# Queries and keys of both attention branches: seven quadrant products in place of eight in a transformer layer's input projection

## The chip, the core and the metric

One core of one Trainium2 chip runs the whole layer in one launch. The metric is device time in microseconds (us). The kernel before took 2883.06 us (median of 3 runs, 2879.89 to 2885.41).

Names: PE is TensorE (matrix products; "PEld" is its load of stationary weights), DVE is VectorE, ACT is ScalarE, POOL is GpSimd, SP is SyncE, which here only issues DMAs. SBUF is the on-chip memory with 128 partitions, PSUM the memory that PE writes its sums to. `T` = 1024 tokens, `D` = 1024 features, `TC` = 256 context tokens, `P` = 128.

## What is computed

The reference is one layer of a diffusion transformer with two attention branches. Cut to what matters here:

```
x  = layer_norm(x, ...) * (1 + sc1) + sh1          # 1024 tokens x 1024
xc = layer_norm(ctx, ...) * (1 + sc1c) + sh1c      # 256 tokens x 1024
p, pc = x @ w_in, xc @ w_in                        # w_in: 1024 x 11264
qr, kr, vr, gr, qd, kd, vd, gate_r, gate_d = split(p)
qr, kr, qd, kd = rope(qr), rope(kr), rope(qd), rope(kd)
... chunked retention on qr, kr, vr; differential attention on qd, kd, vd;
... gates, output projection, layer norm, gated feed-forward, layer norm
```

The context rows of the keys (`kr`, `kd`) are projected too and not rotated; queries have no context rows. All products keep close to fp32 precision: each operand is split into a high part (`h`, rounded to the matmul type fp32r) and a low part (`l` = x - h), and three matmuls h*h + h*l + l*h stand for one (`mm3`).

## The kernel before, in words

The program is written as straight Python loops. A scheduler orders the instructions of each engine before the launch, by its own estimate of times, and each engine then runs its list in that order. So an instruction that waits holds up all that is behind it on its engine.

**First stage (L324 to L397).** Eight blocks of 128 tokens of x are loaded, normalised on DVE and POOL, transposed on PE into `xn` (features on partitions, 8 tiles k of 128 x 1024 tokens). Then, for each k, `mod_both` loads 1 MB of `w_mod` by SP and makes scale and shift; POOL applies them to `xn[:, k]` (L396), and `split` (L84: a copy on ACT, a subtraction on DVE) makes `xH[:, k]` and `xL[:, k]` (L397). These stay in SBUF for all projections.

**Projections (L435 to L658).** The columns of `w_in` are taken in groups of 256. For one group `w_cols` (L233) loads two raw tiles `wraw` of 128 x 1024 (four k tiles of 256 columns each) and splits them into the ring of weight tiles `wh`, `wl` (3 raw buffers, 6 of each split tile). `proj_T` (L456) makes one half of a group, 128 columns by 1024 tokens: for each of 8 k tiles, 3 matmuls by 2 cuts of 512 tokens, so 48 matmuls into `px` (PSUM, 128 x 1024); where the context is wanted, 24 more of 256 tokens into `pcx`. A group has two halves. Then `rope` (L468) makes four products of `px` with the cosine and sine tables on DVE, reading PSUM, and POOL does one subtraction and one addition (L477, L478), each 128 x 1024. The differential branch (`proj_dif`, L481) splits each result again and stores it by 16 DMAs of 32 rows on ACT's queue (L497); the retention branch (`proj_ret`, L499) stores it by 2.

The order is QD (4 groups), KD (4, with context), VD (2 groups of 512 columns, `proj_N`, with x as the stationary operand), QR (4), KR (4, with context), VR (4 of 512). The very first group of QD (`proj_first`, L447) takes its k tiles as the first stage delivers them. `context` (L536) normalises the context rows behind the first group; its PE work is 16 transposes into the small PSUM banks (`ptc`). `decays` (L561) makes tables for the retention branch on DVE and ACT.

**Later.** Attention with the projection of the gates beside it, retention, output projections, the feed-forward. The feed-forward's up projection (L1196 to L1400) already makes its products by seven quadrant products in place of eight, with the same order of products 1, 2, 6, 5, 7, 3, 4, a ring of 3 raw and 4 split buffers, four POOL subtractions of 128 x 512 per tile of weights, and copies from PSUM by ACT.

PSUM has two small tiles of one bank each (`small_ps`) and three of two banks (`big_ps`).

Of the kernel before, what the change touches and what calls it, by code (L numbers as in the profile page):

```python
# [16 lines left out]
P = 128  # L17
# [47 lines left out]
def build(nc, tc, A, out, upto=99, dbg=None):  # L65
# [45 lines left out]
    d_row = dram("d_row", [2, D])  # L111

# [159 lines left out]
    def mod_both(pool, raw, segs):  # L272

        tiles = mod_load(raw, segs)
        pm = small_ps("pm")[:, 0:256]
        for s in range(2):
            for i in range(4):
                k = 2 * i + s
                PE.matmul(pm[32 * i:32 * i + 32, :], condT[:, k, :], tiles[k // 4][:, k % 4, :],
                          start=s == 0, stop=s == 1, tile_position=(0, 32 * i))  # L280
        md = pool.tile([P, 256], F32, name="md", tag="md", bufs=2)
# [36 lines left out]
    open_ring("wring1", 3, 6)  # L318
# [4 lines left out]
    with ExitStack() as ph:  # L323
        wp = ph.enter_context(tc.tile_pool(name="p0", bufs=1))  # L324
# [23 lines left out]
        def norm_pair(src, b0, dst, stats):  # L348
            xb = []
            for b in (b0, b0 + 1):  # L350
                t = ring["pool"].tile([P, D], F32, name="xb", tag="wl" if b < 6 else "wh", bufs=ring["bufs"])
# [39 lines left out]
        for k in range(KT):  # L391
            mod_both(wp, lambda i: ring["pool"].tile([P, 1024], F32, name="mr", tag="wh", bufs=ring["bufs"]), (k, 8 + k))
# [42 lines left out]
    with ExitStack() as ph:  # L435
        wp = ph.enter_context(tc.tile_pool(name="p1", bufs=1))
        ropex = ExitStack()
        rp = ropex.enter_context(tc.tile_pool(name="rope", bufs=1, side="right"))
# [8 lines left out]
        def proj_first(ws):  # L447
# [6 lines left out]
            return [(p, None) for p in px]  # L454

        def proj_T(ws, view, want_ctx):  # L456

            px = big_ps("px")
            for k in range(KT):
                mm3(px, (view(ws[k][0]), view(ws[k][1])), (xH[:, k, :], xL[:, k, :]), T, k == 0, k == KT - 1)  # L460
            pc = None
            if want_ctx:
                pc = small_ps("pcx")[:, 0:TC]
                for k in range(KT):
                    mm3(pc, (view(ws[k][0]), view(ws[k][1])), (cH[:, k, :], cL[:, k, :]), TC, k == 0, k == KT - 1)
            return px, pc

        def rope(pa, pb):  # L468
            t = [rp.tile([P, TK if i in (0, 2) else T], F32R, name=f"rp{i}", tag=f"rp{i}", bufs=2 if i in (0, 2) else 1)
                 for i in range(4)]  # L470
            full = t[0], t[2]
            t = [x.bitcast(F32)[:, :T] for x in t]
            tt(t[0], pa, trig["cos"], ALU.mult)
            tt(t[3], pa, trig["sin"], ALU.mult)
            tt(t[1], pb, trig["sin"], ALU.mult)
            tt(t[2], pb, trig["cos"], ALU.mult)
            tt(t[0], t[0], t[1], ALU.subtract, G)  # L477
            tt(t[2], t[2], t[3], ALU.add, G)  # L478
            return full

        def proj_dif(c0, g, dst, want_ctx):  # L481
            if c0 == C_QD and g == 0:
                pq = proj_first(ws0)
            else:
                ws = w_cols(w_in, c0 + g * 256, 256, perm=perm_dif)
                pq = [proj_T(ws, lambda w: w[:, half * P:half * P + P], want_ctx) for half in range(2)]
            for half, l in enumerate(rope(pq[0][0], pq[1][0])):
                h = rp.tile([P, TK], F32R, name="dh", tag="dh", bufs=2)
                split(h[:, :T], l[:, :T], l[:, :T].bitcast(F32))
                n = T  # L490
                if want_ctx:
                    split(h[:, T:], l[:, T:], pq[half][1])
                    n = TK
                for i in range(4):
                    for part, src in ((0, h), (1, l)):
                        r0 = part * 64 + half * 32
                        ST.dma_start(out=dst[4 * g + i, r0:r0 + 32, :n], in_=src[32 * i:32 * i + 32, :n].bitcast(F32))  # L497

        def proj_ret(c0, g, dst, want_ctx):  # L499
            ws = w_cols(w_in, c0 + g * 256, 256)  # L500
            pq = [proj_T(ws, lambda w: w[:, half * P:half * P + P], want_ctx) for half in range(2)]
            for half, tsrc in enumerate(rope(pq[0][0], pq[1][0])):
                ST.dma_start(out=dst[g, half, :, :T], in_=tsrc[:, :T].bitcast(F32))
                if want_ctx:
                    cs = wp.tile([P, TC], F32, name="cs", tag="cs", bufs=2)
                    S.copy(out=cs, in_=pq[half][1])
                    ST.dma_start(out=dst[g, half, :, T:], in_=cs)

# [11 lines left out]
        def proj_N(c0, dst, d0, want_ctx, func):  # L520

            ws = w_cols(w_in, c0, 512)
            for b in range(0, 10 if want_ctx else 8, 2):
# [6 lines left out]
                st = wp.tile([P, 2, 512], F32, name="st", tag="st", bufs=2)  # L530
# [5 lines left out]
        def context():  # L536

            cst = wp.tile([P, 2, 2], F32, name="cst")
            cn = [wp.tile([P, 4, TC], F32, name="cn%d" % i, tag="st", bufs=2) for i in range(2)]
            xb = []  # L540
            for b in range(2):
                t = ring["pool"].tile([P, D], F32, name="xc", tag="wl", bufs=ring["bufs"])
# [18 lines left out]
        def decays():  # L561


            small = wp.tile([P, 1024], F32, name="small", tag="st", bufs=2)
# [61 lines left out]

        with tc.issue_after(turns["mod"]):
            trig_tables("dif")
        for g in range(4):
            with tc.issue_after(turns["mod"]) if g == 1 else ExitStack():  # L630
                proj_dif(C_QD, g, d_qd, False)
            if g == 0:
                with tc.issue_after(turns["mod"]):
                    context()
            if g == 1:
                decays()
        for g in range(4):
            proj_dif(C_KD, g, d_kd, True)
        for g in range(2):
            proj_N(C_VD + g * 512, d_vd, g * 512, True, AF.Copy)  # L640
        trig_tables("ret")
        for g in range(4):
            proj_ret(C_QR, g, d_qr, False)
        for g in range(4):
            proj_ret(C_KR, g, d_kr, True)
        ropex.close()
# [10 lines left out]
        for g in range(4):  # L657
            proj_N(C_VR + g * 512, d_vr, g * 512, True, AF.Copy)  # L658
    bigx.close()
# [852 lines left out]
```

## Time and profile before

| what | value |
|---|---|
| runs | 2883.06 us median (2879.89 to 2885.41) |
| the profiled execution | 2888.07 us, of which its profile spans 2886.3 us |
| PE busy | 2793.8 us, 97% of the span |
| DVE, ACT, POOL busy | 56%, 39%, 28% |
| PE's granted clock | 0.988 of full speed over the span |
| first stage | 0 to about 71 us, its end mixed with the first group |
| QD and KD | about 71 to 247 us |
| VD, QR, KR, VR | about 247 to 359, to 446, to 557, to 780 us |

How to read it: times in the rows are us from the start of the profile's span, those of single instructions ns where marked. "Busy" of PE counts overlapping matmuls, since they are pipelined; the rate at which PE works is the distance of one start to the next. A wait is named by the engine that released it.

### The profile page before, as it was taken

The page shows a single profiled execution, that of the slowest core. Times are in us where ns is not written, and L with a number is a line of the kernel's source. Part 1 is how long each engine was busy: PE and PEld are TensorE (multiplying, and loading weights), DVE is VectorE, ACT ScalarE, POOL GpSimd, SP SyncE. Part 2 cuts the span into 40 slices and gives each one's busy share as a digit, 9 for nine tenths or more (in the row PEclk, how much of TensorE's full clock was granted, in tenths as well). Part 3 has the DMA queues.
Part 4 walks back from the last instruction along what each step waited for, and adds up shares of the span by engine and source line. Part 5 has one row for each costly group of instructions (what it writes and reads, how often), then busy time and mean ns, then how long its engine had stood idle before and what let it go on. Part 6 is the DMA issues. An engine that isn't in the chain of part 4 may idle for free.

```text
span 2886.3 us, 34740 instructions
## 1 busy us (share of the span) xinstructions
PE 2793.8 (97%) x13610; PEld 2327.8 (81%) x13610; DVE 1626.6 (56%) x2139; ACT 1122.6 (39%) x1570; POOL 809.8 (28%) x613
## 2 busy tenths in 40 slices
PE   7999999999999999999998999899998999999997
PEld 5888888888788888888886877788776788888876
DVE  4864243322167766777758775333556555557666
ACT  4321211111144545544546767433345444444221
POOL 3321022100000000000027764234442333337744
PEclk9999999999999999999999999999999999999999
DMA  8755332453233332323233433643321322224421
GB/s 250 212 165 168 125 124 79 132 175 110 70 92 92 112 95 93 108 91 103 65 113 107 140 115 113 236 150 120 118 89 52 110 81 88 81 81 168 138 95 59
DMA packets 261476, 340.18 MB, mean 118 GB/s; under 512 B 15479, under 2 KB 192064, under 8 KB 261312
## 3 DMA queue, kind: packets, MB, share of 16 engines
q1 hardware_dynamic: 222992, 258.50, 28.7%
q10 hardware_dynamic: 38320, 79.46, 7.8%
q8 instruction: 107, 1.75, 0.3%
q14 instruction: 57, 0.47, 0.1%
HBM read 242.73 MB, written 95.17 MB: 117 GB/s over the span
## 4 chain that ended last, share of the span: by engine, by line
PE 81%; DMA 5%; DVE 5%; POOL 3%; ACT 3%; issue 3%; SPq 0%; ACTq 0%; DVEq 0%; POOLq 0%
PE pg L253 18%; PE pxn L253 11%; PE px L253 11%; PE pu L253 8%; PE py L253 8%; PE pyd L253 6%; PE sp L717 5%; PE po L253 4%; PE pxo L253 2%; PE tp L741 2%; PE pcx L253 2%; DMA g<-d_gT 1%; DVE acc L71 1%; PE pS L253 1%; DMA wraw<-in_w_in 1%
## 5 line engine op out<-in xcount | busy, mean ns | idle before, releaser
L71 DVE TENSOR_TENSOR wl<-wraw,wh 128x1024 fp32r<-128x1024 f32 (+1 forms) x233 | 319.8, 1386 | 248.1 <-ACT wh L85 241.5
L85 ACT CAST wh<-wraw 128x1024 fp32r<-128x1024 f32 (+1 forms) x233 | 218.7, 947 | 473.0 <-PE pu L253 107.9
L71 POOL TENSOR_TENSOR rd<-ident,wh 128x512 fp32r<-128x512 f32 x16 | 18.2, 1137 | 860.6 <-ACT wh L85 827.0
L720 DVE TENSOR_SCALAR_CACHE_REDUCE e<-sp 128x1280 f32<-128x1280 f32 x128 | 190.5, 1489 | 107.2 <-PE sp L717 106.5
L82 ACT ACTIVATE e<-e,m 128x1280 f32<-128x1280 f32 x128 | 175.0, 1367 | 184.0 <-DVE e L720 183.6
L71 POOL TENSOR_TENSOR wraw<-wraw 128x512 f32<-128x512 f32 x85 | 148.9, 1752 | 266.7 <-DVE wl L71 254.3
L71 POOL TENSOR_TENSOR rp<-rp,rp 128x1024 f32<-128x1024 f32 x32 | 89.0, 2804 | 379.4 <-DVE rp L71 359.7
L253 PE MATMUL pg<-xH,wh 128*128 128x512 f32 x496 | 194.9, 393 | 0.0
L253 PE MATMUL pg<-xH,wl 128*128 128x512 f32 x496 | 194.7, 393 | 0.0
L253 PE MATMUL pg<-xL,wh 128*128 128x512 f32 x496 | 194.4, 392 | 0.0
L717 PE MATMUL sp<-ks,qd 128*128 128x512 f32 (+1 forms) x768 | 174.4, 362 | 1.5 <-DVE e L720 1.4
L253 PE MATMUL py<-opH,wh 128*128 128x512 f32 x384 | 150.9, 398 | 10.0 <-DVE ga L71 6.0
L253 PE MATMUL px<-xL,wh 128*128 128x512 f32 x512 | 158.2, 390 | 0.0
L253 PE MATMUL px<-xH,wl 128*128 128x512 f32 x512 | 157.7, 389 | 0.0
L253 PE MATMUL px<-xH,wh 128*128 128x512 f32 x512 | 156.8, 391 | 0.0
L253 PE MATMUL py<-opL,wh 128*128 128x512 f32 x384 | 152.1, 396 | 1.0 <-DVE opL L71 1.0
L253 PE MATMUL pxn<-wh,xH 128*128 128x512 f32 x384 | 151.1, 394 | 0.0
L253 PE MATMUL py<-opH,wl 128*128 128x512 f32 x384 | 150.8, 394 | 0.0
L253 PE MATMUL pxn<-wh,xL 128*128 128x512 f32 x384 | 149.6, 390 | 0.0
L253 PE MATMUL pxn<-wl,xH 128*128 128x512 f32 x384 | 149.4, 389 | 0.0
L717 PEld LDWEIGHTS sp<-ks,qd 128*128 128x128 f32 x768 | 129.3, 188 | 24.6 <-DVE e L720 4.2
L81 ACT ACTIVATE st<-pxn 128x1024 f32<-128x1024 f32 x30 | 30.8, 1027 | 235.0 <-PE pxn L253 231.0
(356 smaller groups left out, 7166.7 us busy)
## 6 DMA issues: line engine op xcount, KB each, us to landing
wraw<-in_w_in SPq DMA_DIRECT2D x88, 512.0 KB
wraw<-in_w_up SPq DMA_DIRECT2D x44, 512.0 KB
mr<-in_w_mod SPq DMA_DIRECT2D x32, 512.0 KB
qd<-d_qd SPq DMA_DIRECT2D x128, 128.0 KB
ga<-d_ga SPq DMA_DIRECT2D x24, 512.0 KB
d_u<-u SPq DMA_DIRECT2D x22, 512.0 KB
fl<-d_u SPq DMA_DIRECT2D x22, 512.0 KB
wraw<-in_w_down SPq DMA_DIRECT2D x22, 512.0 KB
```

The source lines that it names most:

```text
L71: eng.tensor_tensor(out=o, in0=a, in1=b, op=op)
L81: return S.activation(out=o, in_=a, func=func, bias=bias, scale=scale)
L82: return S.activation(out=o, in_=a, func=func, bias=bias, scale=scale, accum_out=accum)
L85: S.copy(out=h, in_=x)
L253: PE.matmul(ps[:, c:e], w, m[:, c:e], start=start and i == 0, stop=stop and i == 2, skip_group_check=more)
L717: st["pe"] = PE.matmul(sp[:, a:b], w, r["k"][c][:, a:b], start=part == 0, stop=part == 1).ins
L720: V.tensor_scalar(out=e, in0=sp[:, :TK], scalar1=-0.125, scalar2=None, op0=ALU.mult, op1=ALU.min, accum_out=m)
L741: PE.transpose(tp[:, k, :], a[:, k * P:(k + 1) * P], ident)
```

## The change

What it does:

- 15 of the 16 groups of QD, KD, QR and KR (all but the first) go through `proj_pair`. Both the group (1024 features x 256 columns) and x (1024 features x 1024 tokens) are cut into quadrants: two halves of features, two halves of columns or tokens. Seven products of 512 features, 128 columns and 512 tokens (products 1, 2, 6, 5, 7, 3, 4) make the four quadrants of the result, with sums of quadrants of weights and of x as operands.
- The sums of the weights are made per group on POOL (four subtractions of 128 x 512), and 7 or 8 half tiles are split where 4 were. The sums of x are made in the first stage for k = 4 to 7, two steps on POOL and two on DVE per k, and three splits of 128 x 512 per k. The sum that takes the place of the quadrant a21 is written over `xH` and `xL` after the first group; the original goes out to `d_a21` and comes back before VD.
- Products are put together in SBUF: four copies from PSUM on ACT and three additions on DVE that read PSUM, each 128 x 512. `rope` then reads SBUF and works in place.
- The context rows of KD are stored by DMAs of their own (16 more per group).
- The ring has 4 split buffers in place of 6; several tiles share buffers with others (`xb`, `mr`, `cn`, `xc`, `md`).
- Order: QD, KD, QR, KR, then the reload of `xH`, `xL`, `decays`, VD, VR. `context` comes after the third group in place of the first, and its tiles are in the buffers of the rotation (`rt0`, `rt1`).

With `NP = 0` no gates are made here. Cut to its core:

```diff
-    open_ring("wring1", 3, 6)
+    open_ring("wring1", 3, 4)
...
             split(xH[:, k, :], xL[:, k, :], xn[:, k, :])
+            if k < 4:
+                continue
+            j = k - 4
+            a11, a12, a21, a22 = xn[:, j, t_lo], xn[:, k, t_lo], xn[:, j, t_hi], xn[:, k, t_hi]
+            tt(a11, a11, a21, ALU.subtract, G)
+            split(xs[7][0][:, j, :], xs[7][1][:, j, :], a11)
+            tt(a21, a21, a22, ALU.add)
+            tt(a22, a22, a11, ALU.subtract)
+            split(xs[6][0][:, j, :], xs[6][1][:, j, :], a22)
+            tt(a12, a12, a22, ALU.subtract, G)
+            split(xs[3][0][:, j, :], xs[3][1][:, j, :], a12)
...
+            u, v = [rp.tile([P, T], F32R, name="rt%d" % i, tag="rt%d" % i, bufs=2) for i in range(2)]
+            t0, t1, p0, p1 = [x.bitcast(F32) for x in (u, v, pa, pb)]
+            tt(t0, p0, trig["cos"], ALU.mult)
+            tt(t1, p1, trig["sin"], ALU.mult)
+            tt(p0, p0, trig["sin"], ALU.mult)
+            tt(p1, p1, trig["cos"], ALU.mult)
+            tt(t0, t0, t1, ALU.subtract, G)
+            tt(p0, p0, p1, ALU.add, G)
...
+        def weights_1(f):
...
+            W[f] = {"raw": raw, "h0": ring_split(raw[0], perm, None if ctx else (0,))}
+            tt(b11, b12, b11, ALU.subtract, G)
+            tt(b12, b22, b12, ALU.subtract, G)
+        def weights_2(f):
...
+            W[f]["h1"] = ring_split(raw[1], perm)
+            b21, b22 = [in_order(raw[1], perm, i) for i in range(2)]
+            tt(b22, b22, in_order(raw[0], perm, 0), ALU.subtract, G)
+            tt(b21, b21, b22, ALU.subtract, G)
+            W[f]["t0"] = ring_split(raw[0], perm)
+        def weights_3(f):
+            W[f]["t1"] = ring_split(W[f]["raw"][1], todo[f][1])
...
+        def product(ps, f, n, first):
+            w, at = W[f][places[n][0]], places[n][1]
+            for k in range(4):
+                mm3(ps, [x[:, at + k * P:at + k * P + P] for x in w], operand(n, k), 512, first and k == 0, k == 3, more=not first)
+        def proj_pair(f):
+            c0, perm, ctx, finish, args = todo[f]
+            side = big_ps("pg")
+            chain, p2, p5 = small_ps("px", f % 2), side[:, t_lo], side[:, t_hi]
+            out = out_tiles()
+            a, b = [x.bitcast(F32) for x in out]
+            product(chain, f, 1, True)
+            S.copy(out=a[:, t_lo], in_=chain)
+            product(p2, f, 2, True)
+            tt(a[:, t_lo], a[:, t_lo], p2, ALU.add)
+            product(chain, f, 6, False)
+            S.copy(out=b[:, t_lo], in_=chain)
+            product(p5, f, 5, True)
+            S.copy(out=b[:, t_hi], in_=p5)
+            product(chain, f, 7, False)
+            tt(b[:, t_hi], b[:, t_hi], chain, ALU.add)
+            if f + 1 < len(todo):
+                weights_1(f + 1)
+            product(p5, f, 3, False)
+            tt(b[:, t_lo], b[:, t_lo], p5, ALU.add)
...
+            product(chain, f, 4, False)
+            S.copy(out=a[:, t_hi], in_=chain)
+            if f + 1 < len(todo):
+                weights_2(f + 1)
+                weights_3(f + 1)
+            finish(*args, out, pc)
...
+        first = proj_first(ws0)
+        with tc.issue_after(turns["mod"]):
+            weights_1(1)
+            weights_2(1)
+            weights_3(1)
+        for i, x in enumerate((xH, xL)):
+            ST.dma_start(out=d_a21[i], in_=x[:, 0:4, t_hi].bitcast(F32))
+        for k in range(4):
+            split(xH[:, k, t_hi], xL[:, k, t_hi], xn[:, k, t_hi])
...
+        for f in range(1, len(todo)):
+            if todo[f][0] == C_QR:
+                trig_tables("ret")
+            proj_pair(f)
+            if f == 2:
+                context()
+        for i, x in enumerate((xH, xL)):
+            SP.dma_start(out=x[:, 0:4, t_hi].bitcast(F32), in_=d_a21[i])
...
+        decays()
         for g in range(2):
             proj_N(C_VD + g * 512, d_vd, g * 512, True, AF.Copy)
```

## Rows read from the trace of the kernel before

**Rows 1.** The page, busy time by engine, and PE over the span in 40 slices.

```profile
PE 2793.8 (97%) x13610; PEld 2327.8 (81%) x13610; DVE 1626.6 (56%) x2139; ACT 1122.6 (39%) x1570; POOL 809.8 (28%) x613
...
PE   7999999999999999999998999899998999999997
```

**Rows 2.** Busy time by stage: first; QD, KD; QR; KR; the up projection.

```profile
core 0: us, PE busy (x) PEld busy (x) DVE busy (x) ACT busy (x) POOL busy (x), PEclk, DMA share, GB/s
0.00:62.00 62.00, 43.09 (x299) 31.44 (x300) 31.16 (x75) 25.57 (x40) 25.28 (x47) 0.97 0.89 265
71.00:247.00 176.00, 174.33 (x867) 148.09 (x866) 123.83 (x164) 47.94 (x87) 51.30 (x25) 1.00 0.59 176
...
359.00:446.00 87.00, 87.00 (x388) 72.07 (x387) 34.66 (x32) 9.47 (x9) 17.21 (x6) 1.00 0.36 120
446.00:557.00 111.00, 111.00 (x581) 95.75 (x580) 41.66 (x26) 10.98 (x16) 24.62 (x9) 1.00 0.24 80
...
2262.00:2620.00 358.00, 358.00 (x1560) 292.62 (x1559) 204.76 (x188) 152.43 (x190) 131.99 (x75) 1.00 0.27 86
```

**Rows 3.** Waits of PE, 71 to 780 us (total, times, longest).

```profile
PE ptc L553 <- POOL xc L74: 1.7, 1, 1.7
```

**Rows 4.** PE in order of time, QR and the first of KR: start us, us, instruction.

```profile
399.75 0.62 PE L253 MATMUL px<-xH,wl 128*128 128x512 f32 x2
...
403.38 0.62 PE L253 MATMUL px<-xL,wh 128*128 128x512 f32 x2
...
457.33 0.28 PE L253 MATMUL pcx<-cH,wh 128*128 128x256 f32 x1
...
459.96 0.28 PE L253 MATMUL pcx<-cL,wh 128*128 128x256 f32 x1
```

**Rows 5.** POOL by tile, up projection and QR, KR: ns min/median/max.

```profile
L71 POOL TENSOR_TENSOR wraw<-wraw x73: 1289/1307/2327, 2260.9 to 2609.9; 128x512 f32<-128x512 f32 x73
...
L71 POOL TENSOR_TENSOR rp<-rp,rp x16: 2402/2894/3393, 382.7 to 557.7; 128x1024 f32<-128x1024 f32 x16
```

**Rows 6.** Groups of DVE and of ACT in the up projection, shapes apart (busy us, mean ns).

```profile
L71 DVE TENSOR_TENSOR wl<-wraw,wh 128x1024 fp32r<-128x1024 f32 x52 | 62.1, 1220 | 5.9 <-ACT wh L85 5.9
L71 DVE TENSOR_TENSOR ug<-ug,pg 128x512 f32<-128x512 f32 x17 | 11.7, 688 | 46.8 <-PE pg L253 46.8
L71 DVE TENSOR_TENSOR wl<-wraw,wh 128x512 fp32r<-128x512 f32 x17 | 11.6, 684 | 0.0
...
L85 ACT CAST wh<-wraw 128x512 fp32r<-128x512 f32 x17 | 10.5, 620 | 41.2 <-PE pu L253 41.2
...
L1382 ACT COPY ur<-pu 128x512 f32<-128x512 f32 x17 | 9.9, 584 | 0.0
```

**Rows 7.** DVE, then POOL, in order of time in QR (start us, us).

```profile
404.27 1.21 DVE L71 TENSOR_TENSOR rp<-px,cos 128x1024 f32<-128x1024 f32 x1
405.40 2.52 DVE L71 TENSOR_TENSOR wl<-wraw,wh 128x1024 fp32r<-128x1024 f32 x1
...
404.43 5.74 POOL L71 TENSOR_TENSOR rp<-rp,rp 128x1024 f32<-128x1024 f32 x2 [16.02 <-DVE rp L71]
```

**Rows 8.** By tile, QD and KD: issues on ACT's queue, results' splits, ns min/median/max.

```profile
L497 ACTq DMA_DIRECT2D d_kd<-rp x24: 308/438/1357, 175.2 to 233.8; - x24
...
L85 ACT CAST dh<-rp x14: 1037/1054/1059, 84.5 to 229.5; 128x1024 fp32r<-128x1024 f32 x14
L71 DVE TENSOR_TENSOR rp<-rp,dh x14: 1208/1216/1414, 90.9 to 230.5; 128x1024 fp32r<-128x1024 f32 x14
L71 DVE TENSOR_TENSOR rp<-pcx,dh x7: 409/416/425, 165.5 to 234.9; 128x256 fp32r<-128x256 f32 x7
```

**Rows 9.** First stage: POOL's scaling of x tile k = 4, DVE's split of k = 7.

```profile
49.03 1.20 POOL L74 TENSOR_SCALAR xn<-xn,aff 128x1024 f32<-128x1024 f32 x1 [3.07 <-DVE aff L77]
...
72.66 1.23 DVE L71 TENSOR_TENSOR xL<-xn,xH 128x1024 fp32r<-128x1024 f32 x1 [6.94 <-ACT xH L85]
```

**Rows 10.** POOL on the context's tiles: ns min/median/max.

```profile
L74 POOL TENSOR_SCALAR cn<-cn,aff x8: 557/1226/2294, 89.0 to 97.6; 128x256 f32<-128x256 f32 x8
```

**Rows 11.** PE in order of time, second tile of the up projection.

```profile
2246.96 0.50 PE L253 MATMUL pu<-s6h,wh 128*128 128x512 f32 x1 [2.28 <-ACT ur L1268]
...
2247.99 0.60 PE L253 MATMUL pu<-s6l,wh 128*128 128x512 f32 x1
...
2250.94 0.62 PE L253 MATMUL pu<-s6h,wl 128*128 128x512 f32 x1
```

More of the change, by code (lines that the diff above doesn't have):

```diff
@@ L468, in rope @@
-        def rope(pa, pb):
[L469 to L493, printed above, removed]
+            return px
@@ L494, in proj_dif, with out_tiles, send_dif @@
+        def out_tiles():
+            return [rp.tile([P, T], F32R, name="p" + n, tag="p" + n, bufs=2) for n in "ab"]
+        def send_dif(g, dst, res, n, at=0):
+            for half, (l, h) in enumerate(res):
+                split(h, l, l.bitcast(F32))
                 for i in range(4):
@@ L496, in proj_dif @@
                         r0 = part * 64 + half * 32
[L497 to L506, printed above, removed]
-                    ST.dma_start(out=dst[g, half, :, T:], in_=cs)
+                        ST.dma_start(out=dst[4 * g + i, r0:r0 + 32, at:at + n], in_=src[32 * i:32 * i + 32, :n].bitcast(F32))
@@ new lines, in finish_dif, with finish_ret @@
+        def finish_dif(g, dst, out, pc):
+            send_dif(g, dst, rope(*out), T)
+            if pc is not None:
+                cs = [[wp.tile([P, TC], F32R, name="c" + n, tag="md", bufs=4) for n in "lh"] for i in range(2)]
+                for i in range(2):
+                    S.copy(out=cs[i][0].bitcast(F32), in_=pc[:, i, :])
+                send_dif(g, dst, cs, TC, T)
+        def finish_ret(g, dst, out, pc):
+            for half, (t, _) in enumerate(rope(*out)):
+                ST.dma_start(out=dst[g, half, :, :T], in_=t.bitcast(F32))
+            if pc is not None:
+                for half in range(2):
+                    cs = wp.tile([P, TC], F32, name="cs", tag="md", bufs=4)
+                    S.copy(out=cs, in_=pc[:, half, :])
+                    ST.dma_start(out=dst[g, half, :, T:], in_=cs)
@@ new lines, in build, with ring_split @@
+        W = {}
+        def ring_split(raw, perm, only=None):
+            pair = [ring["pool"].tile([P, 1024], F32R, name="w" + n, tag="w" + n, bufs=ring["bufs"]) for n in "hl"]
+            if perm or only is not None:
+                for s in range(2) if only is None else only:
+                    c = slice(512 * s, 512 * s + 512)
+                    split(as_raw(pair[0][:, c], perm), as_raw(pair[1][:, c], perm), in_order(raw, perm, s))
+            else:
+                v = raw.rearrange("p (a s c) -> p s a c", a=4, s=2)
+                split(*[x.rearrange("p (s a c) -> p s a c", s=2, a=4) for x in pair], v)
+            return pair
@@ L627, in build @@
+        p0x.close()
+        ropex = ExitStack()
+        rp = ropex.enter_context(tc.tile_pool(name="rope", bufs=1, side="right"))
         with tc.issue_after(turns["mod"]):
             trig_tables("dif")
[L629 to L636, printed above, removed]
@@ L637, in build @@
-        for g in range(4):
-            proj_dif(C_KD, g, d_kd, True)
+        pair0 = out_tiles()
+        for o, p in zip(pair0, first):
+            S.copy(out=o.bitcast(F32), in_=p)
+        finish_dif(0, d_qd, pair0, None)
+        for f in range(1, len(todo)):
[6 more added lines that the diff above has]
+            SP.dma_start(out=x[:, 0:4, t_hi].bitcast(F32), in_=d_a21[i])
@@ L658, in build @@
             proj_N(C_VR + g * 512, d_vr, g * 512, True, AF.Copy)
+    p1x.close()
     bigx.close()
```

101 lines of the change are left out of this document (72 added, 29 removed).

## The prediction

> **What bounds the kernel now.** I read the page first: PE is busy for 97% of the span and for 9 tenths or more in nearly every slice after the first [rows 1]. Then the table by stage: from QD to KR PE is busy for all but 1.7 us, at full clock, while DVE reaches 70% in QD and KD and POOL 29% [rows 2]. The list of PE's waits shows that only one is there between 71 and 780 us, 1.7 us for the context's transposes [rows 3]. So in the projections the number of matmuls sets the time. Their price is the distance of starts, not the 390 ns that a row shows: from 399.75 to 403.38 us there are 16 matmuls of 512 columns, 0.2269 us each; from 457.33 to 459.96 us 22 of 256 columns, 0.1195 us each [rows 4]. A group was 96 x 0.2269 = 21.8 us, with context (48 x 0.1195 = 5.7) 27.5 us.
>
> **The change part by part.** The sum is made against the profiled execution, 2888.07 us, which is 5.0 above the median of the runs.
>
> (a) *Fewer matmuls.* A pair takes 7 products x 4 tiles x 3 = 84 in place of 96: 12 fewer in 15 groups, 180 x 0.2269 = **-40.8 us**. The context's matmuls stay. A group becomes 19.1 us, with context 24.8.
>
> (b) *What has to fit beside them.* Prices, alone: POOL's subtraction of 128 x 512 1.31 us and its step of the rotation 2.40 (the fastest; the median of 2.89 is under contention) [rows 5]; a weight split on DVE 0.68 per half tile, 1.22 per whole one; a DVE addition from PSUM 0.69; on ACT 0.62 for a half tile's copy and 0.58 for a copy from PSUM [rows 6]; an issue on ACT's queue 0.44, a result's copy 1.05 and its split on DVE 1.22, of the context 0.42 [rows 8].
>
> POOL and DVE can't be counted apart. At 404.43 us POOL began two steps of 2.40; a weight split of 1.22 that DVE began at 405.40 took 2.52, and the two steps 5.74 in place of 4.80. From 404.43 to the end there are 5.74 us against 6.02 for all three in a row. The product before it, which reads PSUM, took its usual 1.21 beside POOL [rows 7]. So a DVE operation with two SBUF operands and a POOL operation take turns, one that reads PSUM doesn't join. No row shows the rotation reading SBUF, as the change makes it. It either stays free (then a QD group's turns are 17.2 us and hidden) or joins like the weight split. I take the second, since the weight split is the nearest row, with two SBUF operands of the same shape.
>
> The Trainium skill, "SBUF — State Buffer", section "Who interferes with whom", states that a DVE instruction with two SBUF inputs contends with a GpSimd instruction that reads SBUF, whole instruction by whole instruction, and that one with a single SBUF input does not. By it the rotation joins, which is the second case; had it stayed outside, the sum would be 13 us lower (QD 9, QR 4).
>
> Turns per group, POOL 4 x 1.31 + 2 x 2.40 = 10.0 in each:
> - QD (3 groups): weights 7 x 0.68 = 4.8, rotation 4 x 1.22 = 4.9, results 2 x 1.22 = 2.4; in all 22.1 against PE's 19.1. **+3.0 x 3 = +9** (0 to 15).
> - KD (4): 8 x 0.68 = 5.5 + 4.9 + 2.4 + 0.8 + 10.0 = 23.6 against 24.8. ACT: 32 issues (16 before) 14.0, 8 copies of weights 5.0, 4 from PSUM 2.3, results 2.1, context about 1.5: 24.9. No room on ACT, little on DVE. **+0.7 x 4 = +3** (0 to 14).
> - QR (4): 0.7 + 3 x 1.22 + 4.9 + 10.0 = 19.3 against 19.1, full without a pause. **+1 x 4 = +4** (0 to 11).
> - KR (4): 4.9 + 4.9 + 10.0 = 19.8 against 24.8: hidden, +0 (0 to 4).
>
> The up projection is the pattern with room: POOL 5.2 and DVE 11 of 19 us per tile, and no waits [rows 2, 6]. There the same four copies and three additions cost nothing, because product 2, 5 or 3 (2.7 us) lies between a result and the product that goes on in its bank. In the projections that cover holds as long as DVE and ACT are not late.
>
> (c) *Sums of x in the first stage.* For each of k = 4 to 7: POOL 2 x 1.31, DVE five of 0.68, 6.0 of turns, on top of the tile's own split of 1.23 [rows 9]. k = 4 is scaled at 49.0 us. From there 4 x (6.0 + 1.2) = 29 and the first pair's weights (4.8 + 5.2 = 10) end at 88 us if all go in a row. PE wants the sums at product 6 of the first pair: KD ends at 247, less 3 x 21.8 and 4 x 27.5 is 71.6, plus products 1 and 2 (5.4) 77 us. So 0 to +11, and I take **+6**, the middle: DVE was only half busy here [rows 2], but the last tile's split (at 72.66) was held 6.9 us by ACT's list, which may go better or again so. The write of 2 MB to DRAM, the new split of the a21 quadrant (4 x 0.68 on DVE) and the loads of the tables come before product 5 of that pair is due and wait for nothing else: 0, or 3 if DVE is still behind.
>
> (d) *The context, later and in the rotation's buffers.* `xc` needs the second buffer of `rt1`, which the third group's results hold until their stores land: about 15 us of rotation and splits and 7 of issues after that group's end. Then statistics, 16 transposes, eight POOL steps of 0.56 alone, median 1.23 [rows 10] (5 to 10 us), and splits (2 x 1.22): some 40 us, and KD's first context matmul is due 19.1 + 16.3 = 35 us after. **+4** (0 to 15).
>
> (e) *Order.* `decays` has nothing on PE, and VD's first four token blocks (4 x 24 x 0.2269 = 21.8 us) read tokens below 512, which the reload doesn't touch. SP queues the reload behind KR's weights, ahead of VD's: 0 (0 to 4), hidden by those blocks; if SP were late, VD's first split would be. With 4 split buffers VD's weights wait for the last token block, as in the up projection's ring: 0.
>
> (f) *PE's clock.* After 2.28 us of idling at 2246.96 us PE ran on, and from 2247.99 to 2250.94 us eight matmuls started 0.43 us apart, the distance at 1.2 GHz, in place of 0.23 at 2.4 GHz: 1.6 us more [rows 11]. Two such falls: **+3** (0 for none, 18 if each pair of QD, KD and QR has one).
>
> Sum: -40.8 + 9 + 3 + 4 + 6 + 4 + 3 = **-12**, so 2876 for an execution like the profiled one, and on the footing of the median 2883.06 - 12 = **2871 us**.
>
> **Rivals.**
>
> *PE stays the bound.* The turns are hidden, because QD's excess of 9 us is put off into KR's room of 5 us per group, and only some of (c) is left. For it: the up projection without a wait. Against it: the next pair's weights stand behind the old pair's rotation on DVE, so little can be put off. -41 + 4: 2846 us.
>
> *The context or the first stage takes the rest.* (c) and (d) at their upper ends, 11 + 15 in place of 10: +4, 2888 with all else, or 2883 with half of it: no change. For it: the one wait of PE in this stretch was this one [rows 3].
>
> *The lists put the old pair first (slower).* Place: the ACT queue at the change from one pair to the next. The result's last copy, four products, POOL's two steps and the copy of the second result end 0.6 + 4.9 + 4.8 + 1.1 = 11.4 us after product 4. If these casts stand ahead of the next pair's copy of product 1, which product 6 needs after 5.4 us, PE waits 6.0 plus that copy's 0.6 in each of the 7 groups of the differential branch: 46 us in place of (b)'s 12 there. 2871 - 12 + 46 = 2905 us. It decides against the change from 3.4 us per such group. For it: a list that didn't fit held DVE for 6.9 us at 72.66 [rows 9]. Against it: in the up projection copies stand in good order behind ACT's other work.
>
> **How the numbers follow.** Forecast (2857 to 2877) 0.45, PE as the bound 0.19, no change 0.16, slower 0.20. A measurement of this kernel can tell about 0.2% (5.8 us) from no change: faster means below 2877.3, slower above 2888.8. The forecast's range ends at the first and leaves it 0.02. The range of 8 in 10 goes from 2849, which leaves out half of the first rival, to 2899, which leaves out half of the last. Faster 0.62, within 0.2% 0.17, slower 0.21.
>
> **What would show it.** Right: 13430 matmuls in place of 13610; QD pairs of about 22 us, QR of 20, KR of 24.8; PE's waits in QD for DVE's `wl` or ACT's copies; DVE operations of the rotation at 2 us and more beside POOL; a wait of PE near 80 us for the sums of x. Wrong: no waits of PE (the first rival); waits for the copy of product 1 of some 6 us per pair (the last); or a loss elsewhere, in VD or after it, which nothing above accounts for.

## The result, and the profile after

The kernel after takes 2925.47 us (median of 4 runs, 2924.05 to 2927.82), the kernel before beside it 2884.01. The ratio is 1.0147, with an interval of 1.0129 to 1.0165: slower by some 41 us, where I forecast 12 us faster. The profiled execution took 2925.68 us, its span is 2923.8.

The page of the kernel after, busy time and the strips in 40 slices:

```profile
PE 2770.1 (95%) x13430; PEld 2303.1 (79%) x13430; DVE 1724.1 (59%) x2249; ACT 1197.2 (41%) x1697; POOL 916.5 (31%) x681
...
PE   6679899999999999999998999899898999999997
...
PEclk9889999999999999999998999999999999999999
```

PE has the 180 matmuls less, and of the first five slices three that were at 9 tenths in [rows 1] have come down: the loss stands at the front. The table by stage says where (PE's busy time is the second number):

```profile
0.00:71.00 71.00, 47.54 (x302) 33.49 (x303) 46.60 (x86) 31.10 (x49) 32.27 (x53) 0.90 0.79 247
71.00:97.00 26.00, 16.12 (x57) 12.25 (x57) 21.54 (x27) 10.69 (x17) 15.70 (x10) 0.80 0.23 78
...
140.00:174.00 34.00, 8.91 (x36) 6.36 (x34) 16.41 (x23) 8.34 (x12) 13.69 (x12) 0.68 0.36 108
174.00:298.00 124.00, 119.89 (x611) 102.26 (x610) 83.07 (x87) 43.77 (x78) 51.89 (x29) 0.99 0.46 127
298.00:485.00 187.00, 177.90 (x840) 148.44 (x841) 115.80 (x88) 51.57 (x72) 96.30 (x44) 0.96 0.35 118
485.00:823.00 338.00, 335.68 (x1489) 274.18 (x1488) 102.03 (x226) 63.30 (x84) 5.79 (x2) 1.00 0.45 151
```

Up to 174 us PE idles, and its clock is down (0.80, 0.68) where [rows 2] had 1.00. From 485 us on, V is as it was. The list of PE's waits from 71 to 486 us (total, times, longest), where [rows 3] had one line:

```profile
PE ptc L661 <- POOL xc L74: 21.3, 1, 21.3
PE px L254 <- ACT pa L589: 8.5, 2, 5.7
PE px L254 <- DVE wl L71: 8.3, 4, 3.9
PE px L254 <- ACT xH L85: 8.2, 1, 8.2
...
PE px L254 <- ACT pb L593: 3.0, 4, 1.2
```

**The ledger.** In the kernel before, QD, KD, QR and KR end at 557 us with 112 us of VD in between [rows 2]: 445 us for them and the first stage. Less 40.8, KR's last matmul (556.5 us before) would start at about 404. It starts at 485.0, so 81 us were lost. The starts of product 6 in PE's order of time split them:
- pair 1 at 97.2 us, where 77 was due: **20** (first stage);
- from pair 2 (119.5) to pair 3 (174.0) 54.5 us in place of 19.1: **35.5** (context);
- the other thirteen steps and KR's end: **26**. Those of QD and KD are 3.1, 3.4, 1.7, 0.1, 0.9 and -0.1 above 19.1 or 24.8, those of QR 2.3, 6.6, 1.0 and 4.3, KR's 2.9 in all.

Of the 35.5, 21.3 is the wait at the context's transposes and 3.8 these themselves; 6.4 are shorter waits, and about 4 go with matmuls that start 0.43 us apart in place of 0.23. The 77 us leaves out that the kernel before has the transposes in that stretch too, 1.7 us of waiting [rows 3] and 1.7 for the 16 of them; counted with these, PE was due at some 73.6, the first stage lost about 24 us and the context about 32.

What follows KR takes 2439 us (before 2886 - 445 = 2441). So -41 + 81 - 2 is 38, against 37.5 between the spans.

**The context.** The kernel after in order of time, by engine (start us, us):

```profile
140.67 0.39 PE L254 MATMUL pg<-xH,wl 128*128 128x512 f32 x1
162.32 3.78 PE L661 MATMUL ptc<-ident,xc 128*128 128x128 f32 x16 [21.26 <-POOL xc L74]
...
148.33 3.62 ACTq L497 DMA_DIRECT2D d_qd<-rt  x8
...
131.39 0.34 SPq L651 DMA_DIRECT2D xc<-in_ctx  x1
...
153.35 0.34 SPq L651 DMA_DIRECT2D xc<-in_ctx  x1
...
157.92 1.29 DVE L155 BATCH_NORM_STATS2 lnc_st<-xc 128x6 f32<-128x512 f32 x2 [3.62 <-DMA xc<-in_ctx]
...
161.06 2.37 POOL L74 TENSOR_SCALAR xc<-xc,lnc_rs,cst 128x1024 f32<-128x1024 f32 x2 [9.31 <-DVE cst L77]
```

PE stands at the transposes from 140.9 to 162.3 us. Read it backwards: POOL's scaling waits for the statistics, these for the second load of `xc`, issued at 153.35, when the stores of pair 2's first result (issues to 152.0) had left the buffer. The first load had gone out 22 us earlier. In PE's list product 2 of pair 3 (the row at 140.67 is its last matmul) stands ahead of the transposes, product 1 behind them.

**The first stage.** DVE and POOL, the scaling of block 7:

```profile
75.14 0.15 DVE L71 TENSOR_TENSOR mcol<-pc,pcol 128x4 f32<-128x4 f32 x1
...
79.74 1.22 DVE L74 TENSOR_SCALAR one<-mcol 128x2 f32<-128x2 f32 x1
...
83.73 0.22 DVE L74 TENSOR_SCALAR aff<-one,pcol 128x2 f32<-128x2 f32 x1
...
84.18 2.77 POOL L74 TENSOR_SCALAR xn<-xn,aff 128x1024 f32<-128x1024 f32 x1 [1.52 <-DVE aff L77]
```

Four tiny steps take 9 us, because splits and sums stand between them; before, that scaling began at 65.8 us.

### The profile page after: what moved, and what is told of

It is laid out like the page before. It is cut to its first block, busy times and chain, and to the rows that moved or that the text cites. A ratio compares the mean times of both kernels' runs of the same rounds, so it can differ in the third digit from the quotient of the medians.

```text
span 2923.8 us, 34861 instructions
## 1 busy us (share of the span) xinstructions
PE 2770.1 (95%) x13430; PEld 2303.1 (79%) x13430; DVE 1724.1 (59%) x2249; ACT 1197.2 (41%) x1697; POOL 916.5 (31%) x681
## 5 line engine op out<-in xcount | busy, mean ns | idle before, releaser
L71 DVE TENSOR_TENSOR wl<-wraw,wh 128x1024 fp32r<-128x1024 f32 (+1 forms) x274 | 328.5, 1212 | 238.8 <-ACT wh L85 234.7
L85 ACT CAST wh<-wraw 128x1024 fp32r<-128x1024 f32 (+1 forms) x274 | 248.2, 917 | 400.8 <-PE pu L254 107.6
L71 POOL TENSOR_TENSOR wraw<-wraw 128x512 f32<-128x512 f32 x145 | 246.7, 1701 | 382.5 <-DVE wl L71 374.3
L254 PE MATMUL pg<-xH,wl 128*128 128x512 f32 x616 | 241.6, 392 | 1.7 <-DVE wl L71 1.7
L254 PE MATMUL pg<-xH,wh 128*128 128x512 f32 x616 | 241.9, 393 | 0.2 <-DVE pa L71 0.2
L254 PE MATMUL pg<-xL,wh 128*128 128x512 f32 x616 | 241.4, 392 | 0.0
L254 PEld LDWEIGHTS pg<-xH,wl 128*128 128x128 f32 x616 | 115.8, 188 | 27.0 <-DVE wl L71 2.1
L254 PEld LDWEIGHTS pg<-xH,wh 128*128 128x128 f32 x616 | 115.9, 188 | 25.4 <-DVE pa L71 0.4
L254 PEld LDWEIGHTS pg<-xL,wh 128*128 128x128 f32 x616 | 115.9, 188 | 21.0
L71 DVE TENSOR_TENSOR atl<-tp,ath 128x1280 fp32r<-128x1280 f32 x64 | 95.1, 1486 | 15.5 <-ACT ath L85 15.3
```

Source lines behind the costliest of these rows:

```text
L71: eng.tensor_tensor(out=o, in0=a, in1=b, op=op)
L85: S.copy(out=h, in_=x)
L254: PE.matmul(ps[:, c:e], w, m[:, c:e], start=start and i == 0, stop=stop and i == 2, skip_group_check=more)
```

## The experiments

Each kernel is timed beside the kernel before. What comes after KR took 2436 to 2451 us in these kernels, although no edit concerns it: the scheduler makes other lists for the whole program each time. So I read each edit by two numbers, the total and the start of KR's last matmul.

| kernel | median us | ratio to before (95%) | KR's last matmul |
|---|---|---|---|
| after | 2925.5 | 1.0147 (1.0129 to 1.0165) | 485.0 |
| e1 context claims first | 2910.1 | 1.0084 (1.0067 to 1.0101) | 466.8 |
| e2 context before pair 0 ends | 2928.1 | 1.0155 (1.0140 to 1.0170) | 487.3 |
| e5 sums in a second loop | 2929.0 | 1.0155 (1.0140 to 1.0170) | 487.5 |
| e6 no sums | 2932.1 | 1.0164 (1.0149 to 1.0179) | 484.8 |
| f1 = e1, old pair behind copies | 2966.4 | 1.0285 (1.0269 to 1.0300) | 521.1 |
| f2 = e1, POOL's six steps on DVE | 2901.5 | 1.0061 (1.0046 to 1.0076) | 451.3 |
| f3 = e1, no sums, same memory | 2897.2 | 1.0050 (1.0031 to 1.0069) | 457.8 |
| f4 = e1, sums listed last | 2926.5 | 1.0152 (1.0136 to 1.0168) | 487.8 |
| g2 = e1, four stores for sixteen | 2975.4 | 1.0308 (1.0293 to 1.0323) | 530.2 |
| g1 = f2, four stores for sixteen | 2980.0 | 1.0330 (1.0312 to 1.0347) | 531.4 |
| g3 = f2, second group plain | 2893.7 | 1.0025 (1.0015 to 1.0035) | 440.9 |
| g4 = g1 and g3 together | 2951.9 | 1.0227 (1.0212 to 1.0243) | 512.4 |
| h5 = after, stores from SP | 2936.0 | 1.0174 (1.0159 to 1.0190) | 492.4 |
| h3 = e1, stores from SP | 2921.3 | 1.0122 (1.0102 to 1.0142) | 475.6 |
| h1 = f2, stores from SP | 2891.8 | 1.0021 (1.0012 to 1.0030) | 441.8 |
| **h2 = g3, stores from SP** | **2872.5** | **0.9953 (0.9940 to 0.9967)** | 432.2 |
| k2 = h2, weights back on POOL | 2896.2 | 1.0033 (1.0021 to 1.0045) | 443.1 |
| k3 = h2, rotation back on POOL | 2899.4 | 1.0044 (1.0031 to 1.0056) | 445.5 |

**The context's buffer: e1, e2.**

```
e1, in proj_pair:                        e2, in the main sequence:
+ if f == 2:                             + context()
+     context()                            finish_dif(0, d_qd, pair0, None)
  finish(*args, out, pc)                   ...
- (the call after proj_pair(2))          - (the call after proj_pair(2))
```

> The context's two loads take the rope's buffers before pair 2's rotated results do, at the same place of the list; pair 2's rotation and stores come after. Theory 'buffer' (the idle stretch of 21.3 us ahead of ptc stands there because the second load of xc waits for pair 2's stores to land): the wait falls to under 6 us, total 2905 to 2911. Rival 'chain' (the load, the statistics, the normalising and the scaling of the context take that long by themselves wherever the buffer comes from): the wait stays at 15 us or more, total 2920 to 2930. Second rival 'moved': pair 2's rotation and stores, now behind the context, hold pair 4's output tiles, the wait on ptc goes but 8 us or more come back in pairs 3 and 4, total 2914 to 2922.

> The whole context is issued ahead of the rotation of pair 0, where all of the rope's buffers are still free. Theory 'buffer': no wait on a store is left, the 21.3 us ahead of ptc go, total 2902 to 2910. Rival 'first stage is the tight place' (DVE, POOL and ACT are the bound from 71 to 140 us): the context's 8 POOL and DVE steps push pairs 1 and 2 back by as much as is saved, total 2918 to 2930.

In e1 the wait at `ptc` falls from 21.3 to 2.0 us. PE's waits there, from 71 to 467 us:

```profile
PE px L254 <- ACT pa L589: 11.2, 4, 7.8
...
PE px L254 <- ACT pb L593: 5.4, 4, 3.7
PE pg L254 <- ACT pb L595: 4.7, 2, 3.9
...
PE ptc L663 <- POOL xc L74: 2.0, 1, 2.0
```

KR's last matmul comes 18.2 us earlier and the total falls by 15: theory "buffer". The step from pair 2 to 3 falls from 54.5 to 31.9 us, which is still 12.8 over 19.1. What returns is in the copies (`pa`, `pb`). In e2 the wait shrinks too, to 11.4 us, but now stands at 93.5 us in the full first stage. Pair 3's product 6 starts at 160.3 in place of 174.0, yet by pair 6 the lead is gone (247.5 against 247.9): the rival held. Here a free buffer was not enough.

**The first stage: e5, e6, f3, f4, g3.** e5 makes the sums in a loop of their own after the eight blocks; f4 does that on top of e1 and orders DVE, POOL and ACT to issue them behind block 7's scaling and cast. e6 and f3 leave out the sums and their splits, and f3 keeps their memory reserved.

```
e5, f4:                                  e6, f3, in operand():
- if k < 4:                              - if n in xs:
-     continue                           -     return [x[:, k, :] for x in xs[n]]
+ for k in range(4, KT):                 + {6: (0, t_lo), 7: (0, t_lo), 3: (4, t_lo), ...}[n]
```

> The sums of x and their splits are issued after all eight blocks are scaled and split, in place of in turn with blocks 4 to 7. Theory 'order' (the first projection waits for block 7 because the sums of blocks 4 to 6 stand ahead of it on DVE, ACT and POOL): the wait 'px <- ACT xH' of 8.7 us falls under 3, product 6 of pair 1 starts at 85 to 92 in place of 97.2, total 2913 to 2920. Rival 'amount' (the sums' work has to be done before product 6 in any order): the first projection ends earlier but product 6 waits as long, start 96 to 99, total 2922 to 2928.

> Leaves out the sums of x and their splits: products 6, 7 and 3 read quadrants of x itself. Theory 'sums' (their work and order cost the first stage 20 us): product 6 of pair 1 at 77 to 82, total 2903 to 2910. Rival 'buffers' (the first stage is late because the ring has 4 buffers in place of 6, and the modulation's weights arrive 8 us later): product 6 of pair 1 at 87 or later, total 2914 or more.

> On top of the context's claim first (2910 us): leaves out the sums of x and their splits, products 6, 7 and 3 read quadrants of x, the memory of the sums stays reserved so that no later stage starts earlier. Theory 'sums': product 6 of pair 1 starts at 80 to 86 in place of 97.7, and with the context's buffer out of the way this is kept: total 2892 to 2900. Rival 'pacing' (pairs 1 and 2 are paced by DVE, POOL and the arrival of weights, so they end where they did): total 2905 to 2913.

> On top of the context's claim first (2910 us): the sums of x are listed on DVE, POOL and ACT behind block 7's scaling and cast, now by an explicit order of the lists (the second loop of the source alone had left DVE's list as it was, instruction for instruction). Theory 'order': block 7's cast ends by 76 in place of 88 us, the wait of 8.2 us for xH goes, product 6 of pair 1 starts at 87 to 92, total 2900 to 2906. Rival 'amount': product 6 of pair 1 starts at 96 or later, total 2908 to 2915.

e5 tells nothing on the order: the scheduler put DVE's list of the first stage back as it was. e6 is no clean test either: without the sums' memory the tables of `decays` moved into the first stage (DVE, ACT), product 6 of pair 1 starts at 87.0, behind a wait of 6.2 us for a copy, and the context's wait (22.1 us) took what was won; it is why f3 keeps the memory and stands on e1. There the sums' absence gives 9.0 us at KR's end and 13 in the total, as the theory had it. Product 6 of pair 1, first in e1, then in f3:

```profile
97.71 0.39 PE L254 MATMUL px<-x6h,wh 128*128 128x512 f32 x1
```

```profile
79.66 0.50 PE L254 MATMUL px<-xH,wh 128*128 128x512 f32 x1 [0.63 <-ACT pa L581]
```

At that place the sums cost 18 us, with the same number of ring buffers, so e6's rival "buffers" explains little. By product 6 of pair 3 (144.9 in place of 153.9 us) half of it is gone again, in waits for ACT's copies and for DVE.

f4 shows that this other order is no better. Block 7 is done earlier, but product 6 of pair 1 starts at 116.6 in place of 97.7 us: PE waits 10.6 us for the copy of pair 0's result and up to 8.5 for `wl`, which now stand behind the sums. That is the rival's side, the amount of work, and dearer than I wrote; that no order of the lists would do better is not shown.

g3 lets PE run while that work is done: the second group too is made with eight products, before the a21 quadrant is overwritten, so the third group is the first to need the sums. It costs 12 matmuls, 2.7 us.

```
  first = proj_first(ws0)
+ then = proj_second(w_cols(w_in, C_QD + 256, 256, perm=perm_dif))
...
- weights_1(1); weights_2(1); weights_3(1)
+ weights_1(2); weights_2(2); weights_3(2)
```

> On top of the kernel with POOL's six operations on DVE (2901 us): the second query group too is made with eight products (12 matmuls more, 2.7 us), so the sums of x are first read by the third group. Theory 'sums too late' (they end some 15 us after PE wants them): PE runs on while they are made, the stretch to the third group's product 6 shortens by 10 to 15 us, total 2889 to 2896. Rival 'pacing' (DVE has as much to do either way, and what is not waited for here is waited for in the next pairs): 2898 to 2906.

10.4 us earlier at KR's end, 7.8 less in the total. One wait of 16.0 us is left: pair 2's copy of product 1, behind the casts and issues of both groups before it, one of which (`d_qd<-pa`) waited for DVE's low part.

**POOL beside DVE: f2, k2, k3.** f2 takes `G` from the two sums of the rotation and from the four subtractions of weights.

```
- tt(t0, t0, t1, ALU.subtract, G)        - tt(b11, b12, b11, ALU.subtract, G)
+ tt(t0, t0, t1, ALU.subtract)           + tt(b11, b12, b11, ALU.subtract)
  (and p0)                                 (and b12, b22, b21)
```

> On top of the context's claim first (2910 us): the four subtractions of weights and the two sums of the rotation of each pair go from POOL to DVE (6 operations, 4 x 0.68 + 2 x 1.22 = 5.2 us more on DVE per pair, 10 us less on POOL). Theory 'turns' (DVE and POOL exclude each other, so POOL's 10 us per pair are taken from DVE): DVE's operations return to 0.68 and 1.22 us, the pairs' excess over 19.1 and 24.8 us falls by half or more, total 2892 to 2902. Rival 'DVE has no room': DVE's own list of 22 us per pair, now without POOL's help, is longer than PE's 19.1: total 2908 to 2920.

DVE by groups, shapes apart, from 150 to 310 us (busy us, mean ns), first e1, then f2:

```profile
L71 DVE TENSOR_TENSOR wl<-wraw,wh 128x512 fp32r<-128x512 f32 x34 | 26.7, 819 | 4.0 <-ACT wh L85 4.0
L71 DVE TENSOR_TENSOR pa<-pa,sin 128x1024 f32<-128x1024 f32 x6 | 15.4, 2558 | 0.0
```

```profile
L71 DVE TENSOR_TENSOR wl<-wraw,wh 128x512 fp32r<-128x512 f32 x35 | 23.2, 693 | 1.2 <-ACT wh L85 1.1
...
L71 DVE TENSOR_TENSOR pa<-pa,sin 128x1024 f32<-128x1024 f32 x7 | 8.5, 1218 | 0.0
```

The product of the rotation that runs beside POOL takes 2558 ns, without POOL 1218. DVE has six operations more per pair and is done sooner: 15.5 us at KR's end, 9 in the total. So the rotation, which now reads SBUF, does join the turns, as I chose in (b). The moved steps are also shorter by themselves on DVE (0.69 us in place of 1.31, 1.22 in place of 2.40); how much of the 15.5 us is that and how much the turns, no run separates.

The Trainium skill, "SBUF — State Buffer", section "Who interferes with whom", states this of a DVE instruction with two SBUF inputs beside a GpSimd instruction that reads SBUF; the two groups above agree.

> The fastest kernel so far (2872 us) with the four subtractions of weights per pair back on POOL; the rotation's sums stay on DVE. Theory 'a result's way is what POOL must stay out of': the weights have a pair's time to spare, so little changes: 2868 to 2878. Rival 'turns, whichever step': 5.2 us of POOL per pair are taken from DVE again: 2880 to 2895.

> The fastest kernel so far (2872 us) with the two sums of the rotation per pair back on POOL; the weights' subtractions stay on DVE. Theory 'a result's way': each sum takes 2.4 to 3.4 us in place of 1.2 on the way from product 4 to the stores that hold SyncE's list and the output tiles, 15 to 20 us in all: 2884 to 2896. Rival 'turns, whichever step': 4.8 of POOL's 10 us per pair come back, like the other kernel within 5 us of it.

Either half on POOL costs about the same, 10.9 and 13.3 us at KR's end (24 and 27 in the total, of which 13 lie after KR, where the lists differ). My theory that only the rotation matters fell. That it is the turns, whichever step takes them, is not shown: 5.5 and 9.9 us of the loss stand in the one step from pair 8 to 9 (26.6 and 31.0 us, in h2 21.1), where SP's lists differ. SP's issue of the weights for pair 9, in h2 and in k2 (k3: 278.04):

```profile
262.87 1.22 SPq L559 DMA_DIRECT2D wraw<-in_w_in  x2
```

```profile
278.12 17.52 SPq L559 DMA_DIRECT2D wraw<-in_w_in  x4
```

In h2 it stands ahead of the 16 stores of the last KD result, in k2 and k3 behind them, and PE waits 3.6 and 3.2 us for `wh`.

**ACT's list: f1, g2, g1, g4, h5, h3, h1, h2.** The kernel after at the change from pair 1 to pair 2, ACT in order of time:

```profile
106.54 4.45 ACTq L497 DMA_DIRECT2D d_qd<-rt  x8
111.03 1.05 ACT L85 CAST pb<-pa 128x1024 fp32r<-128x1024 f32 x1 [4.52 <-POOL pa L71]
...
115.78 0.58 ACT L611 COPY pa<-px 128x512 f32<-128x512 f32 x1 [2.67 <-DMA d_qd<-pa]
116.27 1.66 ACT L85 CAST wh<-wraw 128x512 fp32r<-128x512 f32 x3
118.83 0.58 ACT L589 COPY pa<-px 128x512 f32<-128x512 f32 x1 [0.91 <-DMA d_qd<-pa]
```

The copy of product 1 (L589) at 118.83 stands behind pair 0's casts and 16 issues and three casts of weights; PE waited 5.7 us for it. I tried three ways out. f1 lists the old pair's casts and issues behind the copy of product 5. g2 and g1 store four heads with one transfer. The h kernels issue the stores from SP.

```
f1:  + last = S.copy(out=b[:, t_hi], in_=p5).ins
     + with tc.issue_after(last):
     +     (casts and stores of the pair before)
g2:  - for i in range(4): ... dst[4 * g + i, r0:r0 + 32, at:at + n]
     + dst[4 * g:4 * g + 4, r0:r0 + 32, at:at + n], in_=src[:, :n]
h:   - ST.dma_start(out=dst[4 * g + i, ...      + SP.dma_start(out=dst[4 * g + i, ...
```

> On top of the context's claim first (2910 us): in the differential pairs ScalarE's casts of the rotated results and their 16 to 32 issues are listed behind the next pair's copy of product 5, so they can't stand ahead of its copies of products 1, 6 and 5. Theory 'ACT queue': PE's waits for those copies (21 us in that kernel between 97 and 486 us: pa of product 1 11.2, pb 5.4 and 4.7) fall under 6, total 2894 to 2902. Rival 'DVE and POOL in turns': what PE waits for is only renamed, the waits for wl and wh grow by as much, total 2906 to 2914. Rival 'buffers': the stores come 12 us later, so the output tiles and the rotation's buffers come free later and pairs two further on wait, total 2914 to 2930.

ACT's waits in f1, from 95 to 521 us:

```profile
ACT wh L85 <- POOL wraw L71: 64.7, 19, 9.1
...
ACT pa L625 <- DMA d_kd<-cl: 43.2, 3, 14.7
```

ACT still stands at the issues, 43.2 us in three waits in KD, only later in the pair: the copy of product 4 and the next weights' casts are behind them, and PE waits 33 us for `wh`. The move gave the wait to other work: 54 us later at KR's end.

> On top of the context's claim first (2910 us): each half of a differential result is stored by one transfer of all four heads in place of four, so ScalarE issues 4 (with context 8) in place of 16 (32) per pair, at the same place of its list; bytes are the same. Theory 'ACT queue': the 12 to 24 issues less at 0.44 us free 5 to 11 us of ScalarE per differential pair, PE's 21 us of waits for copies (pa, pb) fall under 8, total 2892 to 2902. Rival 'turns' (the copies are late because the casts ahead of them wait for POOL and DVE, however few the issues): the waits stay within 4 us, total 2906 to 2913.

> The fewer stores on top of the kernel with POOL's six operations of a pair on DVE (2901 us). If both causes are real and separate, the gains add: 2883 to 2893. If they are one and the same wait seen from two sides, 2896 to 2903.

> All edits together: context's claim first, POOL's six operations on DVE, fewer stores, second group plain. If the four causes add up: 2872 to 2884, at or under the kernel of before (2883). If the first stage's work is only put off: 2884 to 2895.

All three came out far slower. ACT in g1 in order of time, and under it the strip of DMA from 180 to 215 us (tenths of 16 engines), g1:

```profile
189.74 1.90 ACTq L496 DMA_DIRECT2D d_qd<-pa  x1
191.73 2.18 ACT L85 CAST wh<-wraw 128x512 fp32r<-128x512 f32 x4 [4.85 <-PE pg L254]
211.29 0.58 ACT L588 COPY pa<-px 128x512 f32<-128x512 f32 x1 [17.38 <-DMA d_qd<-pa]
```

```profile
DMA  0000000224122222222489222222222221100000
GB/s 0 0 0 0 0 0 23 51 61 70 33 56 66 94 112 98 108 112 98 131 282 346 109 106 99 106 105 99 106 100 108 112 98 56 51 14 0 0 0 0
```

Of the sixteen DMA engines two tenths are busy while such a store runs, at about 105 GB/s; it holds its output tile until 211 us, and the copy of product 1 two pairs on needs that tile. With sixteen stores (the kernel after, 106 to 116 us, where only stores of 128 KB move) the strip goes to 9:

```profile
DMA  0000079399480099699798899106889959959798
```

The Trainium skill, "DMA: Bandwidth & Descriptors", section "Why a DMA increments its semaphore by 16 and not by 1", gives the reason: the number of engines is the largest, up to 16, that divides the slowest dimension of both sides, here 4 (heads), where 32 rows allow 16. The strip agrees: 0.2 of 16 is 3 to 4.

> The changed kernel with one edit: the 16 (with context 32) stores of a differential result are issued by SyncE in place of ScalarE. Theory 'issues in line' (ScalarE's list is in order; an issue that waits for DVE's low part, and the 0.44 us of each issue, hold the copies of products behind them): PE's waits for copies (pa, pb) fall from 12 to under 5 us, and pair 2's stores land sooner or later by no more than 5 us, so the context's wait stays; total 2908 to 2918. Rival 'turns' (copies wait because casts wait for POOL and DVE): 2921 to 2928. Rival 'loads' (stores that wait hold the weight loads on SyncE's list): slower, 2930 or more.

> The context's claim first (2910 us) and the stores from SyncE. Theory 'issues in line': 21 us of waits for copies fall to under 8, 2893 to 2902. Rival 'turns': 2906 to 2913.

> Context's claim first, POOL's six operations on DVE (2901 us), and the stores from SyncE. If turns and issues are separate causes: 2882 to 2892. If one covers the other: 2894 to 2902.

> The same with the second group plain (2894 us with ScalarE's stores, where PE stood 16.4 us behind one copy). Theory 'issues in line': that wait goes, 2873 to 2882, faster than both kernels. Rival 'loads': 2886 to 2897.

With POOL in the rotation SP's list is no better: h5 and h3 lose 7.4 and 8.8 us at KR's end. The waits for copies go (12 to 6 us in h5), but the stores wait for late results and hold SP's loads. SP in h5 in order of time:

```profile
305.74 6.12 SPq L497 DMA_DIRECT2D d_kd<-rt  x8
...
317.62 20.60 SPq L549 DMA_DIRECT2D wraw<-in_w_in  x4
```

The next weights go out at 317.6 us, behind the stores and the tables, and the step from pair 8 to 9 takes 37.6 us in place of 21.3. With POOL out of the way the results are early enough, and the same edit gains 9.5 (h1 against f2) and 8.7 us (h2 against g3) at KR's end. Of h2's 21 us on g3 in the total the other 12 lie after KR, where the lists differ. **h2 beats both kernels**: 0.9953 (0.9940 to 0.9967) of the kernel before, and 12.7 us less; its KR ends some 13 us earlier (432 us against the 445 of the ledger). From its list of PE's waits from 0 to 434 us, and two stages of its table:

```profile
...
PE px L254 <- ACT pa L599: 13.7, 2, 13.4
```

```profile
165.00:282.00 117.00, 117.00 (x595) 99.93 (x594) 91.24 (x114) 47.41 (x79) 0.00 (x0) 1.00 0.56 162
282.00:434.00 152.00, 152.00 (x761) 129.42 (x760) 108.23 (x116) 44.80 (x62) 0.00 (x0) 1.00 0.37 125
```

From 165 us on PE has no idle time, as in [rows 2], with 84 matmuls per pair. The one long wait (13.4 us at 102) is again pair 2's copy of product 1, ACT in h2:

```profile
115.39 0.58 ACT L599 COPY pa<-px 128x512 f32<-128x512 f32 x1 [1.77 <-DMA d_qd<-pa]
```

It writes the tile of group 0's second result, whose stores SP issued from 108.0 to 110.1 us, after DVE's low part (to 107.9); DVE works almost without a gap from 94.05 us, when the tables of the rotation had come. What would shorten this was not tried.

## Why the prediction was wrong

- **(a) was right.** 180 matmuls less; in h2 two pairs of QR follow each other by 19.0 us, which is 84 x 0.2269.
- **(d) failed most: +4 (0 to 15) taken, 35.5 measured.** The chain was named rightly, buffer, stores, load, statistics, and its length was about as I had it: from pair 2's product 4 (to 138.3 us) to the end of the context's splits (173.6) 35 us, for some 40. The step that failed is "KD's first context matmul due 35 us after". PE meets the wait not there but at the transposes, which its list had ahead of pair 3's product 1. I had said myself that an instruction that waits holds all behind it, and had not applied it to PE. e1 shows 18 us at KR's end to be the buffer. Listing the transposes later was not tried.
- **(c) failed in size: +6 (0 to 11) taken, 20 measured.** I counted the sums from 49.0 us with DVE and POOL working without a pause, but the last block's small steps stand in the same lists: it is scaled at 84 us. f3 shows that 18 of the 20 us go with the sums where PE first needs them, of which 9 are left at KR's end. The rest goes with the reordered lists and fewer buffers (the modulation's last weights are issued at 58.3 us, before at 50.2); which of these I did not separate. The 77 us that I reckoned from was itself some 3 us late, since it left out the transposes (the ledger). And the one wait of PE near 80 us, 8.2 us from 79.9 on, was for block 7's cast (`xH`) and not yet for the sums.
- **(b) and (f): +19 taken, 26 measured.** QD and KD came close (9.1 us over in six steps). QR has 14 over where I had 4. Of these, 5.8 us are waits, the longest (3.9) for a split of weights that stands behind the rotation in DVE's list and takes 3.36 us beside POOL's sum; 6.8 us go with matmuls that start 0.43 us apart; 1.6 us are context matmuls of KR that were listed early. PE in QR:

```profile
324.56 0.80 PE L254 MATMUL px<-x6h,wl 128*128 128x512 f32 x1 [3.93 <-DVE wl L71]
...
325.58 0.63 PE L254 MATMUL px<-x6l,wh 128*128 128x512 f32 x1
...
329.00 0.63 PE L254 MATMUL px<-xH,wl 128*128 128x512 f32 x1
```

  From 325.58 to 329.00 eight steps take 3.42 us, 0.43 each, the distance at 1.2 GHz. By such distances (f) cost some 10 us in these steps and some 4 in the context's, where I had 3: an estimate from the starts of PE's matmuls. That the rotation takes turns with POOL was right, by f2.
- **(e) was right:** after KR all is as long as before, within what the lists vary.
- **The rival with the ACT list** has its place and its mechanism in the trace, but by 12 us of waits in place of 46. Its remedy is not to move the issues to another point of the list (f1, +54), but to get DVE's results earlier and the stores off ACT (f2, h1).
- **The rival "the context or the first stage takes the rest"** was the case, at twice its upper ends (55.5 in place of 26). Its total was also added up wrongly: 12 less and 16 more make 2887, not 2888, and half of the 16 gives 2879, not 2883.

The range held neither, because I had bounded (c) and (d) by the amount of work, not by where the engines' lists would stop.

Open: how g3's and h2's wait for that one copy could be shortened, what the turns alone cost, and how far the lists after KR (2436 to 2451 us) could be made the better one each time.

## What to carry to other kernels

When work is taken from PE, look for what PE's own list will stop at, not for when the data are used: a prologue's transposes placed between two products make PE wait for the whole chain that feeds them. A tile that waits for stores to land should be claimed before those stores are made, or be another tile. And DVE with POOL is to be counted as one resource where both read SBUF: a DVE product took 2558 ns beside POOL and 1218 without, and moving 10 us of POOL's work per pair onto DVE, as 5 us, brought KR's end 15.5 us forward.

## What I had not expected of the hardware

A store of four times the size was much slower than four stores: some 105 GB/s with two tenths of the DMA engines busy, and 17.4 us of waiting for its tile, which fits a spread over its four heads alone. And the same edit, SP in place of ACT as the issuer, has either sign: +7.4 us at KR's end with POOL in the rotation (h5), -9.5 without (h1).
